# An encoder layer on one core: early sums of squares, a regrouped V for the prompt, V loads in four parts

## The chip, the cores and the metric

The kernel runs on one NeuronCore of one Trainium2 chip, as one launch. The metric is the device time of the launch in microseconds; before the change it is 2137.19 us, the median of three runs (2135.92 to 2137.59).

The engines are named as in the profile: PE is TensorE (PEld its weight loads), DVE is VectorE, ACT is ScalarE, POOL is GpSimd, and SP is SyncE, the engine that issues nearly all DMAs of this kernel, one after the other, on a queue of its own (SPq).

## The reference

One layer of an encoder is applied to a prompt of 512 tokens and to a sample of 2048 tokens, both 1024 wide, in float32 and with shared weights:

```python
def encoder_layer(x, pre_g, post_g, w_in, ...):
    h = rms_norm(x, pre_g)            # x * rsqrt(mean(x*x) + 1e-6) * pre_g
    z = h @ w_in                      # 1024 x (4*512 + 2*256 + 3*256 + 3*1024)
    (q, k, v, gate_a, u_b, gate_b, c_val, c_glu, gate_c,
     merge_a, merge_b, merge_c) = jnp.split(z, split_pts, axis=-1)
    y_a = neighbourhood_attention(heads(q), heads(k), heads(v), rpb) * jax.nn.silu(gate_a)
    y_b = fourier_mix(u_b) * jax.nn.silu(gate_b)
    y_c = conformer_conv(c_val, c_glu, dw_w, dw_b, cn_g, cn_b) * jax.nn.silu(gate_c)
    merged = (jax.nn.sigmoid(merge_a) * (y_a @ w_a) + jax.nn.sigmoid(merge_b) * (y_b @ w_b)
              + jax.nn.sigmoid(merge_c) * (y_c @ w_c))
    return x + rms_norm(merged @ w_o, post_g)
```

The attention sees the tokens as a grid of 64 columns (8 rows for the prompt, 32 for the sample). Each of 8 heads of 64 channels looks at a window of 8 rows by 16 columns, clamped at the border, with a bias by relative position. `fourier_mix` is the real part of a 2-D DFT.

## The kernel before, in words

**Chunks.** The tokens are worked on in five chunks of 512: chunk 0 is the prompt, chunks 1 to 4 are the sample. The order is the chunk pair (1, 2), the pair (3, 4), and then chunk 0 with the merging and the output. A normalized chunk stands in SBUF as eight tiles `hT` of 128 channels by 512 tokens, each split in two parts of a reduced float format, high and low. The weights come in units of 128 x 1024 through `wraw` (three buffers) and are split in the same way into `w` by a cast on ACT and a subtraction on DVE (`split`, L134 and L135). A product is then three matmuls, high by high, high by low and low by high (`narrow`, L178 to L180): 24 matmuls for a block of 512 columns, and one unit serves both chunks of a pair. `unit` keeps three units ready.

**How other work gets among the matmuls.** The projections and the merging run through TensorE in program order. Everything else is a generator that is handed to `task` with a number of steps and a first and last position; after every few matmuls `pump` moves the position on and takes as many steps as are due. The program's order is not the final one: a scheduler of the tile framework orders each engine's instructions by its own model of time, so that where an instruction ends up on DVE, ACT, POOL and SP is seen only in the built program.

**The normalization.** For chunks 1 and 2 the raw x is multiplied and the norm is applied to the products. For chunks 3, 4 and 0 the generator `produce` runs `rstd_rows` and then `make_h`. `rstd_rows` (L199) loads four tiles `xt` of 128 tokens by 1024 through the buffers of `wraw`, squares each on ACT with a sum (L207), gets the reciprocal root by Newton steps on DVE (L126 to L128) and writes it to the DRAM row `rs` (L211). `make_h` (L213) reads that row back, broadcast over the partitions, into `rrow` (L217, one buffer), loads eight tiles `xr` of x transposed (L220, three buffers), multiplies each by `preg` and `rrow` on DVE (L221) and splits it into an `hT`. `produce` of chunks 3 and 4 is a task late in the first pair, that of chunk 0 one late in the second. The tiles of chunk 4 and of chunk 0 take over the eight buffers `ring` of chunk 2 and of chunk 4, those of chunk 3 ten buffers `ring2`.

**The attention.** `attention` (L503) goes over 8 heads and, in each, four blocks `cb` of 16 columns of queries. A block has `nq` x 128 keys: nq is 2 for the prompt, 3 for chunks 1 and 4, 4 for chunks 2 and 3. Per block there are two matmuls for the scores s, a bias (the table `tab` plus a mask, added on POOL at L560 or L563 and made a block ahead), on DVE the sum of both with its maximum (L596), on ACT the exponential (L600), the scaling (L602), then the transposes `pt` (L623), their split into `psp` (L626), and the product `pv` with V (L634), whose halves go into `ob` (L637 and after) and with the last block to DRAM as `ya` (L644, two writes). V comes by `load_v` (L534) at the start of the third block of a head, into `vsp` (two buffers). With nq 4, `grouped`, it takes 8 loads of 16 rows by 8 columns (L540); otherwise 16 loads of 32 keys for nq row groups (L545), four for each block. The prompt's attention runs beside `fft` for chunk 0, which loads `fu` (L664), makes `fab` of it on DVE (L656) and multiplies with the DFT matrix `w` (loaded at L730, 128 x 2048, one buffer; product `hp` at L750).

Of the kernel before, what the change touches and what calls it, by code (L numbers as in the profile page):

```python
# [20 lines left out]
ALU = mybir.AluOpType  # L21
# [13 lines left out]
MASKPAT = (0, 1, 2, 2, 3)  # L35
KSTART = (0, 8, 24, 32)
RCOL = (16, 8, 8, 0)
COLPAT = (0, 1, 1, 2)


def attention_masks():


    out = np.full((4, P, 3, 512), -1e30, np.float32)
    for mp, (rows, r0, kr0, nq) in enumerate(((8, 0, 0, 2), (32, 0, 0, 3), (32, 8, 4, 4), (32, 24, 20, 3))):
        for cp, cb in enumerate((0, 1, 3)):
            for q in range(P):
                r, c = r0 + q // 16, 16 * cb + q % 16
                rs = min(max(r - 4, 0), rows - 8)
                cs = min(max(c - 8, 0), 48)  # L50
                kr = kr0 + np.arange(nq * 4)[:, None]
                kc = KSTART[cb] + np.arange(32)[None, :]
                ok = (kr >= rs) & (kr < rs + 8) & (kc >= cs) & (kc < cs + 16)
                m = np.where(ok, 0.0, -1e30)
                if nq == 4:
                    m = m.reshape(16, 4, 8).transpose(1, 0, 2)
                out[mp, q, cp, : nq * 128] = m.reshape(-1)
    return out.astype(ml_dtypes.bfloat16)

# [44 lines left out]
class Build:  # L104
# [91 lines left out]
                self.pump()  # L196


    def rstd_rows(self, c, pool, xpool, tag, bufs):  # L199

        nc = self.nc
        ss = pool.tile([P, 4], F32, tag="ss", name="ss")
        for i in range(4):
            xt = xpool.tile([P, D], F32, tag=tag, name="xt", bufs=bufs)
            nc.sync.dma_start(xt, self.a["x"][c * C + i * P: c * C + i * P + P, :])
            junk = pool.tile([P, D], BF16, tag="xr", name="junk", bufs=3)
            nc.scalar.activation(junk, xt, AF.Square, accum_out=ss[:, i:i + 1])  # L207
        v = pool.tile([P, 4], F32, tag="v", name="v")
        nc.vector.tensor_scalar(v, ss, 1.0 / D, EPS, op0=ALU.mult, op1=ALU.add)
        r = self.newton(pool, "nr", v, nc.vector)  # L210
        nc.sync.dma_start(self.rs[c].rearrange("o (t p) -> p (o t)", p=P), r)  # L211

    def make_h(self, c, pool, tiles, ring):  # L213

# [289 lines left out]
    def attention(self, c):  # L504
# [2 lines left out]
        nq, trow, krow = PATS[c]  # L507
        n, rows = nq * P, 4 * nq
        kds, vds = self.kds[c > 0], self.vds[c > 0].rearrange("(r w) d -> r w d", w=64)
        grouped = nq == 4  # L510
        mask = pool.tile([P, 3, 512], BF16, tag="mask", name="mask", bufs=1)
        nc.sync.dma_start(mask, self.a["mask"][MASKPAT[c]])
        tq, vq, ahead = [], [], []
# [17 lines left out]
            qk[hh] = ksp, qsp.rearrange("p i (b q) -> p i b q", b=4)  # L531
            tabs[hh] = tb

        def load_v(hh):  # L534

            cols = slice(hh * P, hh * P + P)
            vsp = pool.tile([P, 12, P], F32R, tag="vsp", name="vsp", bufs=2)
            if grouped:
                for g in range(8):
                    nc.sync.dma_start(vsp[:, g].bitcast(F32), vds[krow: krow + rows, 8 * g: 8 * g + 8, cols])  # L540
            else:
                for cb in range(4):
                    for r in range(4):
                        src = vds.rearrange("(q r) w d -> r w q d", r=4)
                        nc.sync.dma_start(  # L545
                            vsp[32 * r: 32 * r + 32, nq * cb: nq * cb + nq].bitcast(F32),
                            src[r, KSTART[cb]: KSTART[cb] + 32, krow // 4: krow // 4 + nq, cols])
            vs[hh] = vsp

        def biases():  # L550
            for hh in range(8):
                for cb in range(4):
                    bias = pool.tile([P, 512], F32, tag="bias", name="bias", bufs=2)
                    g0 = RCOL[cb] // 8
                    t = tabs[hh][:, g0: g0 + 4, trow: trow + rows]
                    m, b = mask[:, COLPAT[cb], :n], bias[:, :n]
                    if grouped:
                        m, b = (x.rearrange("p (g r w) -> p g r w", g=4, w=8) for x in (m, b))
                        m, b, t = (x.rearrange("p g r w -> p g (r w)") for x in (m, b, t))
                        nc.gpsimd.tensor_tensor(b, t, m, op=ALU.add)  # L560
                    else:
                        m, b = (x.rearrange("p (r g w) -> p g r w", g=4, w=8) for x in (m, b))
                        nc.gpsimd.tensor_tensor(b, t, m, op=ALU.add)  # L563
                    yield bias
# [10 lines left out]
        for hh in range(8):  # L575
            ksp, qsp = qk.pop(hh)
            for cb in range(4):
                if cb == 1:
                    load(hh + 1)
                if cb == 2:  # L580
                    load_v(hh)
                if cb % 2 == 0:
                    pv = self.ps.tile([P, 2, 2, P], F32, tag="o", name="pv", bufs=1)
                if cb == 0:
# [3 lines left out]
                s = self.ps.tile([P, 512], F32, tag="s", name="s", bufs=2)  # L588
                kk = ksp.rearrange("p (r c) -> p r c", c=64)[:, :rows, KSTART[cb]: KSTART[cb] + 32]
                if grouped:  # L590
                    kk = kk.rearrange("p r (g w) -> p g r w", w=8)
# [10 lines left out]
                nc.scalar.mul(p[:, :n], p[:, :n], m[:, 3:4])  # L602
                tq.append(partial(self.transpose_p, nq, p, c, hh, cb, vs, pv, obs))
                yield
                if len(tq) > 3:
                    vq.append(tq.pop(0)())
                yield
# [21 lines left out]
    def attend(self, c, hh, cb, nq, vs, psp, pv, obs):  # L629

        nc, vsp, o = self.nc, vs[hh], obs[hh]
        for i in range(nq):
            v = KSTART[cb] // 8 + i if nq == 4 else nq * cb + i
            nc.tensor.matmul(pv[:, cb % 2], lhsT=vsp[:, v], rhs=psp[:, i], start=i == 0, stop=i == nq - 1)  # L634
        if cb % 2 == 0:
            return
        ov = o.rearrange("p (r b c) -> p b r c", r=8, b=4)[:, cb - 1: cb + 1]  # L637
        parts = pv.rearrange("p b i (r c) -> p i b r c", c=16)
        nc.scalar.copy(ov, parts[:, 0])
        nc.vector.tensor_tensor(ov, parts[:, 1], ov, op=ALU.add)  # L640
# [242 lines left out]
    def run(self):  # L883
        tc, nc, a = self.tc, self.nc, self.a
        with ExitStack() as ctx:
# [47 lines left out]

            hT = {c: [] for c in range(NCH)}

            def produce(*cs, x=(self.wraw, "wraw", 3)):
                for c, ring in cs:
                    self.rstd_rows(c, hp, *x)
                    yield
                    yield from self.make_h(c, hp, hT[c], ring)  # L940

            def seq(*gens):
# [33 lines left out]
            second = self.conv(2, cb[2], True)  # L976
            self.task(seq(self.conv(1, cb[1]), islice(second, 20)), 48, base + 20, base + 340)
            self.task(self.dft_parts(), 7, base + 30, base + 200)
            self.proj_qk(hs)
            for g in range(2):  # L980
                self.proj_v(hs, g)
            self.task(self.attention(1), 112, self.pos + 30, self.pos + 270)
            self.proj_u(hs)
            self.gates(hs)
            self.task(produce((3, ring2), (4, ring)), 18, self.pos + 100, self.pos + 292)
            self.merge_gates(hs)
            while len(hT[4]) < KT:
                self.pump()
# [16 lines left out]
            self.task(seq(*(self.attention(c) for c in (2, 3, 4))), 336, self.pos, self.pos + 280)  # L1005
            self.proj_u(hs)
            self.gates(hs)
            self.task(produce((0, ring)), 9, self.pos + 150, self.pos + 232)
            self.merge_gates(hs, turn=True)
            while len(hT[0]) < KT:  # L1010
                self.pump()
# [132 lines left out]
```

## Time and profile before

| | |
|---|---|
| median of three runs | 2137.19 us |
| the profiled execution, its own time | 2136.65 us |
| its span in the trace | 2134.8 us |
| PE busy | 2069.1 us, 97% |
| PEld busy | 1775.8 us, 83% |
| DVE busy | 1300.3 us, 61% |
| ACT busy | 795.8 us, 37% |
| POOL busy | 292.8 us, 14% |
| mean granted clock of TensorE | 0.987 |

The span runs from the first to the last instruction of the trace; the execution's own time is 1.85 us longer. Busy time is a sum over instructions and says nothing of what they waited for. The views read below are the timeline of an engine (each row a run of like instructions, with the idle time before it in brackets and what ended that), the windows (busy time, granted clock and DMA rate of a stretch), and the groups of instructions by line or by tile. The granted clock is given as a share of full speed, 1.00 being 2.4 GHz and 0.50 being 1.2 GHz; a value between is a mean over the stretch. PE is busy for longer in a stretch with a lower clock, for the same work.

### The profile page before, as it was taken

Reading aid. Unit: us, or ns where it says so; the run is one execution under the profiler, and the core shown is the slowest. Engines: PE = TensorE matmul, PEld = TensorE weight load, DVE = VectorE, ACT = ScalarE, POOL = GpSimd, SP = SyncE. Lnnn points to the kernel's source line nnn. Section 1 sums busy time; section 2 is a strip of 40 time slices with the busy share of each in tenths; the row PEclk is TensorE's granted clock in tenths of the full one; section 3 lists DMA queues with packets and bytes.
Section 4 is the critical chain, followed back from the end, with each engine's and each line's share of the span. In section 5 each row is a group of like instructions: output and inputs, shape, how many; then the busy total and the mean of one; then the engine's idle time right before and its main releaser. Section 6 shows DMA issues by size and latency. Waiting matters only on the chain. (4 is left out here: it accounts for less than half of the span.)

```text
span 2134.8 us, 31256 instructions
## 1 busy us (share of the span) xinstructions
PE 2069.1 (97%) x11184; PEld 1775.8 (83%) x11184; DVE 1300.3 (61%) x2850; ACT 795.8 (37%) x1625; POOL 292.8 (14%) x286
## 2 busy tenths in 40 slices
PE   8999999999979999999999969999889999999998
PEld 6889888887867899888888858897778889999997
DVE  6554676556444547686665635887745666666655
ACT  6222243344332215564554635335544311111111
POOL 0000011101000002232221211002100121222211
PEclk9999999999989999999999989999999999999999
DMA  8644444555443536575666676777778765555532
GB/s 299 199 154 162 163 146 147 152 173 159 136 143 115 152 131 177 171 195 173 176 182 185 193 195 193 236 236 219 260 247 300 222 211 173 173 185 171 188 129 77
DMA packets 242091, 389.33 MB, mean 182 GB/s; under 512 B 26784, under 2 KB 140064, under 8 KB 240032
## 3 DMA queue, kind: packets, MB, share of 16 engines
q1 hardware_dynamic: 241936, 387.33, 58.2%
q8 instruction: 89, 1.46, 0.3%
q14 instruction: 66, 0.54, 0.1%
HBM read 284.99 MB, written 109.58 MB: 185 GB/s over the span
## 5 line engine op out<-in xcount | busy, mean ns | idle before, releaser
L178 PE MATMUL mm<-hT,w 128*128 128x512 f32 x1760 | 703.7, 400 | 20.2 <-ACT hT L134 10.9
L180 PE MATMUL mm<-hT,w 128*128 128x512 f32 x1760 | 696.1, 396 | 0.1
L179 PE MATMUL mm<-hT,w 128*128 128x512 f32 x1760 | 695.9, 396 | 0.0
L178 PEld LDWEIGHTS mm<-hT,w 128*128 128x128 f32 x1760 | 333.7, 190 | 88.6 <-ACT hT L134 11.3
L180 PEld LDWEIGHTS mm<-hT,w 128*128 128x128 f32 x1760 | 333.0, 189 | 73.8 <-DVE w L135 1.2
L179 PEld LDWEIGHTS mm<-hT,w 128*128 128x128 f32 x1760 | 333.6, 190 | 66.1 <-DVE hT L242 0.9
L135 DVE TENSOR_TENSOR w<-wraw,w 128x512 fp32r<-128x512 f32 x308 | 222.0, 725 | 176.1 <-ACT w L134 172.3
L134 ACT CAST w<-wraw 128x512 fp32r<-128x512 f32 x308 | 188.5, 618 | 247.3 <-PE mm L180 186.5
L453 DVE SCALAR_TENSOR_TENSOR acc<-cb,cw,acc 128x512 f32<-128x512 f32 (+1 forms) x300 | 237.9, 795 | 2.9
L563 POOL TENSOR_TENSOR bias<-tab,mask 128x384 f32<-128x384 f32 (+1 forms) x96 | 94.3, 984 | 829.7 <-DVE m L596 744.7
L178 PE MATMUL mm<-ysp,wb 128*128 128x256 f32 x640 | 181.1, 283 | 2.7 <-DVE nw_y L116 2.7
L179 PE MATMUL mm<-ysp,wb 128*128 128x256 f32 x640 | 181.0, 283 | 0.0
L180 PE MATMUL mm<-ysp,wb 128*128 128x256 f32 x640 | 180.9, 283 | 0.0
L600 ACT ACTIVATE p<-p,m 128x384 f32<-128x384 f32 (+2 forms) x160 | 102.3, 639 | 184.5 <-DVE m L599 158.6
L596 DVE CUSTOM_DVE_ANT_0 p<-s,bias 128x384 f32<-128x384 f32 (+2 forms) x160 | 92.7, 580 | 86.2 <-PE pt L623 69.2
L560 POOL TENSOR_TENSOR bias<-tab,mask 128x512 f32<-128x512 f32 x64 | 86.1, 1346 | 368.7 <-DVE m L596 356.0
L194 PE MATMUL mm<-w,hT 128*128 128x256 f32 x480 | 134.8, 281 | 0.0
L193 PE MATMUL mm<-w,hT 128*128 128x256 f32 x480 | 134.8, 281 | 0.0
L192 PE MATMUL mm<-w,hT 128*128 128x256 f32 x480 | 134.3, 282 | 0.0
L178 PEld LDWEIGHTS mm<-ysp,wb 128*128 128x128 f32 x640 | 122.4, 191 | 4.3 <-DVE th L831 2.9
L857 PE MATMUL po<-wo,msp 128*128 128x512 f32 x320 | 124.5, 389 | 0.0
L856 PE MATMUL po<-wo,msp 128*128 128x512 f32 x320 | 124.2, 390 | 0.0
(152 smaller groups left out, 2961.7 us busy)
## 6 DMA issues: line engine op xcount, KB each, us to landing
wraw<-wn SPq DMA_DIRECT2D x135, 512.0 KB, 4.5
th<-z SPq DMA_DIRECT2D x120, 256.0 KB, 2.6
th<-th SPq DMA_DIRECT2D x80, 384.0 KB, 3.8
qsp<-qd SPq DMA_DIRECT2D x80, 256.0 KB, 6.2
tab<-tab SPq DMA_DIRECT2D x40, 384.0 KB, 3.9
w<-dftd SPq DMA_DIRECT2D x14, 1024.0 KB, 7.7
vsp<-vds SPq DMA_DIRECT2D x256, 48.0 KB, 2.0
xt<-x SPq DMA_DIRECT2D x20, 512.0 KB, 5.2
```

The lines of the kernel that those rows point to most:

```text
L134: nc.scalar.copy(dst[:, 0], src)
L135: return nc.vector.tensor_tensor(dst[:, 1], src, dst[:, 0].bitcast(F32), op=ALU.subtract)
L178: nc.tensor.matmul(ps, lhsT=u[:, 0, s], rhs=r[:, 0], start=n == 0, stop=False)
L179: nc.tensor.matmul(ps, lhsT=u[:, 0, s], rhs=r[:, 1], start=False, stop=False)
L180: nc.tensor.matmul(ps, lhsT=u[:, 1, s], rhs=r[:, 0], start=False, stop=n == len(kts) - 1)
L192: nc.tensor.matmul(ps, lhsT=r[:, 0, q], rhs=w[:, 0, s], start=kt == 0, stop=False)
L193: nc.tensor.matmul(ps, lhsT=r[:, 0, q], rhs=w[:, 1, s], start=False, stop=False)
L194: nc.tensor.matmul(ps, lhsT=r[:, 1, q], rhs=w[:, 0, s], start=False, stop=kt == KT - 1)
L453: nc.vector.scalar_tensor_tensor(acc[:, :n], cb[:, b, e:e + n], wv[:, e:e + 1], acc[:, :n], op0=ALU.mult, op1=ALU.add)
L600: nc.scalar.activation(p[:, :n], p[:, :n], AF.Exp, bias=m[:, 1:2], accum_out=m[:, 2:3])
L856: nc.tensor.matmul(po, lhsT=r[:, 0, q], rhs=w[:, 0], start=kt == 0, stop=False)
L857: nc.tensor.matmul(po, lhsT=r[:, 0, q], rhs=w[:, 1], start=False, stop=False)
```

## The change

1. `rstd_rows` no longer belongs to `produce`. It is a task of its own, for chunks 3, 4 and 0 in this order, started 20 positions after the first products of chunks 1 and 2 and due by position 200 after them (15 steps). It loads x in halves of 128 x 512 into the three `xr` buffers instead of whole rows into those of `wraw`, squares in place, and adds the two half sums with one more instruction on DVE. `produce` keeps `make_h` alone.
2. The prompt's V is `grouped` too: seven loads of 8 rows by 16 columns (128 keys) that its four blocks share, two blocks each, instead of 16 loads per head. Its keys and its mask are ordered to match, and its bias is added in two POOL instructions of 128 keys.
3. `load_v` works in four parts, two of them in the third block of a head and two in the fourth, for all chunks.

```diff
+VBLOCKS = {4: tuple(range(0, 64, 8)), 2: (0, 16, 8, 24, 40, 32, 48)}
...
-                if nq == 4:
-                    m = m.reshape(16, 4, 8).transpose(1, 0, 2)
+                if nq != 3:
+                    m = m.reshape(4 * nq, nq, 32 // nq).transpose(1, 0, 2)
...
-    def rstd_rows(self, c, pool, xpool, tag, bufs):
+    def rstd_rows(self, c, pool):
 
         nc = self.nc
-        ss = pool.tile([P, 4], F32, tag="ss", name="ss")
+        ss = pool.tile([P, 2, 4], F32, tag="ss8", name="ss8")
         for i in range(4):
-            xt = xpool.tile([P, D], F32, tag=tag, name="xt", bufs=bufs)
-            nc.sync.dma_start(xt, self.a["x"][c * C + i * P: c * C + i * P + P, :])
-            junk = pool.tile([P, D], BF16, tag="xr", name="junk", bufs=3)
-            nc.scalar.activation(junk, xt, AF.Square, accum_out=ss[:, i:i + 1])
+            for k in range(2):
+                xt = pool.tile([P, C], F32, tag="xr", name="xt", bufs=3)
+                row = c * C + i * P
+                nc.sync.dma_start(xt, self.a["x"][row: row + P, k * C: k * C + C])
+                nc.scalar.activation(xt, xt, AF.Square, accum_out=ss[:, k, i:i + 1])
+            yield
         v = pool.tile([P, 4], F32, tag="v", name="v")
-        nc.vector.tensor_scalar(v, ss, 1.0 / D, EPS, op0=ALU.mult, op1=ALU.add)
+        nc.vector.tensor_scalar(v, ss[:, 0], 1.0 / D, EPS, op0=ALU.mult, op1=ALU.add)
+        nc.vector.scalar_tensor_tensor(v, ss[:, 1], 1.0 / D, v, op0=ALU.mult, op1=ALU.add)
...
-        grouped = nq == 4
+        grouped, width = nq != 3, 32 // nq
...
-        def load_v(hh):
+        def load_v(hh, part):
 
             cols = slice(hh * P, hh * P + P)
-            vsp = pool.tile([P, 12, P], F32R, tag="vsp", name="vsp", bufs=2)
+            if part == 0:
+                vs[hh] = pool.tile([P, 12, P], F32R, tag="vsp", name="vsp", bufs=2)
+            vsp, first, last = vs[hh], 2 * part, 2 * part + 2
             if grouped:
-                for g in range(8):
-                    nc.sync.dma_start(vsp[:, g].bitcast(F32), vds[krow: krow + rows, 8 * g: 8 * g + 8, cols])
+                for i, k in enumerate(VBLOCKS[nq][first:last]):
+                    nc.sync.dma_start(vsp[:, first + i].bitcast(F32), vds[krow: krow + rows, k: k + width, cols])
...
+                    elif nq == 2:
+                        for i in range(2):
+                            mi, bi = (x[:, i * P: i * P + P].rearrange("p (r g w) -> p g r w", g=2, w=8)
+                                      for x in (m, b))
+                            nc.gpsimd.tensor_tensor(bi, t[:, 2 * i: 2 * i + 2], mi, op=ALU.add)
...
-                if cb == 2:
-                    load_v(hh)
+                if cb >= 2:
+                    load_v(hh, 2 * cb - 4)
...
                 yield
+                if cb >= 2:
+                    load_v(hh, 2 * cb - 3)
...
-            v = KSTART[cb] // 8 + i if nq == 4 else nq * cb + i
+            v = nq * cb + i if nq == 3 else VBLOCKS[nq].index(KSTART[cb] + 32 // nq * i)
...
-            def produce(*cs, x=(self.wraw, "wraw", 3)):
+            def produce(*cs):
                 for c, ring in cs:
-                    self.rstd_rows(c, hp, *x)
-                    yield
                     yield from self.make_h(c, hp, hT[c], ring)
...
+            self.task(seq(*(self.rstd_rows(c, hp) for c in (3, 4, 0))), 15, base + 20, base + 200)
...
-            self.task(produce((3, ring2), (4, ring)), 18, self.pos + 100, self.pos + 292)
+            self.task(produce((3, ring2), (4, ring)), 16, self.pos + 110, self.pos + 292)
...
-            self.task(produce((0, ring)), 9, self.pos + 150, self.pos + 232)
+            self.task(produce((0, ring)), 8, self.pos + 155, self.pos + 232)
```

What moves is read from the two built programs. Lines of the changed kernel are 2 to 13 higher. First, SP's queue early in the first pair, in the changed program (`xt` are the half rows of x, `rs_100` and `rs_101` the rows of chunks 3 and 4):

```order
L144 DMA wraw<-wn 128x1024 x3
L209 DMA xt<-x 128x512 x3
L144 DMA wraw<-wn 128x1024 x2
L209 DMA xt<-x 128x512 x3
L144 DMA wraw<-wn 128x1024
L209 DMA xt<-x 128x512 x2
L1100 DMA cdf<-cdft 128x256
L209 DMA xt<-x 128x512 x3
L144 DMA wraw<-wn 128x1024
L209 DMA xt<-x 128x512 x7
L216 DMA rs_100<-nw_y 128x4x1
```

The loads of x stand among those of the weights from here to the third row rs, that of chunk 0, 25 rows on; before the change there are weights alone in this place.

Second, SP's queue before the second pair, around the tiles of chunk 4, in the changed program (`rrow<-rs_101` is chunk 4's, `rrow<-rs_97` chunk 0's; `th` are writes of merge gates):

```order
L226 DMA xr<-xT 128x512 x3
L223 DMA rrow<-rs_101 128x512
L444 DMA th_93<-z 128x512
L226 DMA xr<-xT 128x512 x3
L144 DMA wraw<-wn 128x1024
L444 DMA th_94<-z 128x512
L226 DMA xr<-xT 128x512
L144 DMA wraw<-wn 128x1024
L226 DMA xr<-xT 128x512 x2
L444 DMA th_94<-z 128x512
L226 DMA xr<-xT 128x512 x4
L223 DMA rrow<-rs_97 128x512
```

Chunk 0's row is read here, some 600 us of the old trace ahead of its old place, and its first three `xr` follow those of chunk 4.

Third, SP's queue in chunk 0's attention and DFT, before the change:

```order
L545 DMA vsp<-vdp 32x2x128 x4
L644 DMA ya_82<-ob 64x512 x2
L545 DMA vsp<-vdp 32x2x128 x6
L500 DMA yd_77<-th 128x512
L545 DMA vsp<-vdp 32x2x128 x6
L530 DMA tab<-tab 128x768
L664 DMA fu<-ud_72 128x4x128
```

and the same place in the changed program:

```order
L548 DMA vsp<-vdp 128x1x128 x3
L657 DMA ya_82<-ob 64x512 x2
L548 DMA vsp<-vdp 128x1x128 x4
L677 DMA fu<-ud_72 128x4x128
L506 DMA yd_77<-th 128x512
```

Between the writes of `ya` and the load of `fu` there are four V loads where there were twelve, a write and a table.

## Rows read from the trace of the kernel before

**Rows 1.** Timeline of PE, waits over 2 us, 400 to 1620; start, length, instruction, [idle <-releaser]

```profile
500.33 0.98 PE L634 MATMUL pv<-psp,vsp 128*128 128x256 f32 x3 [2.34 <-issue]
...
630.55 0.79 PE L178 MATMUL mm<-hT,w 128*128 128x512 f32 x1 [10.89 <-ACT hT L134]
...
1278.48 0.88 PE L623 MATMUL pt<-ident,p 128*128 128x128 f32 x3 [16.09 <-DVE m L599]
...
1544.18 0.69 PE L623 MATMUL pt<-ident,p 128*128 128x128 f32 x2 [7.90 <-DVE psp L626]
...
1584.91 0.44 PE L623 MATMUL pt<-ident,p 128*128 128x128 f32 x2 [2.08 <-ACT p L602]
...
1590.31 1.01 PE L750 MATMUL hp<-w,fgs 128*128 128x256 f32 x3 [3.65 <-DMA w<-dftd]
```

**Rows 2.** Windows: length, busy PE, PEld, DVE, ACT, POOL, PEclk, DMA share, GB/s

```profile
500.00:505.00 5.00, 4.67 (x15) 3.90 (x16) 4.52 (x9) 1.76 (x4) 0.32 (x1) 0.66 0.48 137
630.00:640.00 10.00, 9.40 (x28) 7.04 (x29) 7.55 (x12) 3.60 (x6) 0.00 (x0) 0.66 0.29 84
1280.00:1285.00 5.00, 5.00 (x23) 4.23 (x22) 3.19 (x11) 3.01 (x7) 0.97 (x2) 0.81 0.63 165
1545.00:1550.00 5.00, 5.00 (x18) 3.97 (x17) 3.05 (x14) 2.98 (x9) 1.36 (x2) 0.68 1.01 383
1590.00:1595.00 5.00, 4.69 (x14) 4.02 (x15) 0.72 (x2) 0.40 (x1) 0.00 (x0) 0.50 0.83 302
```

**Rows 3.** Timeline of DVE, its waits ahead of those of PE

```profile
483.59 0.75 DVE L221 SCALAR_TENSOR_TENSOR xr<-xr,preg,rrow 128x512 f32<-128x512 f32 x1 [10.11 <-DMA rrow<-rs]
...
629.09 1.41 DVE L221 SCALAR_TENSOR_TENSOR xr<-xr,preg,rrow 128x512 f32<-128x512 f32 x2 [12.38 <-DMA rrow<-rs]
...
1274.20 1.41 DVE L221 SCALAR_TENSOR_TENSOR xr<-xr,preg,rrow 128x512 f32<-128x512 f32 x2 [19.58 <-DMA rrow<-rs]
...
1543.03 0.76 DVE L656 TENSOR_TENSOR fab<-fu 128x256 f32<-128x256 f32 x2 [9.93 <-DMA fu<-ud]
```

**Rows 4.** Timeline of SP's queue ahead of C

```profile
1255.60 12.21 SPq L545 DMA_DIRECT2D vsp<-vds  x11
...
1268.33 0.43 SPq L217 DMA_DIRECT2D rrow<-rs  x1
```

**Rows 5.** Timeline of SP's queue ahead of D1 and D2

```profile
1527.83 2.07 SPq L644 DMA_DIRECT2D ya<-ob  x2
...
1533.80 4.34 SPq L545 DMA_DIRECT2D vsp<-vdp  x6
...
1538.66 0.43 SPq L664 DMA_DIRECT2D fu<-ud  x1
...
1574.25 4.59 SPq L545 DMA_DIRECT2D vsp<-vdp  x7
```

**Rows 6.** Timeline of ACT at D2

```profile
1583.83 0.62 ACT L134 CAST w<-wraw 128x512 fp32r<-128x512 f32 x1 [6.05 <-DMA wraw<-wn]
```

**Rows 7.** Instructions of the tile xr, all of the span

```profile
DMA to landing us min/median/max: 2.6/4.6/10.4
```

**Rows 8.** Windows of the early stretch and of chunk 0's attention, columns as in rows 2

```profile
60.00:150.00 90.00, 90.00 (x408) 73.93 (x407) 47.00 (x71) 19.91 (x32) 0.21 (x1) 1.00 0.62 191
1440.00:1535.00 95.00, 93.36 (x485) 77.08 (x484) 77.56 (x215) 55.91 (x144) 19.47 (x21) 1.00 0.76 238
```

**Rows 9.** Instructions of the tile xt, all of the span: ns min/median/max, first and last start

```profile
L207 ACT ACTIVATE junk<-xt x12: 1052/1057/1082, 446.7 to 1241.5; 128x1024 bf16<-128x1024 f32 x12
...
DMA to landing us min/median/max: 3.5/5.2/11.5
```

**Rows 10.** Instructions of the tile wraw, 20 to 120: ended its engine's idle time, us, times

```profile
  PE mm L180: 26.7, 16
```

**Rows 11.** Groups by line and form, POOL, 1300 to 1620: busy us, mean ns

```profile
L563 POOL TENSOR_TENSOR bias<-tab,mask 128x256 f32<-128x256 f32 x32 | 27.5, 863 | 235.9 <-DVE m L596 216.3 <-DVE m L601 11.3 <-DMA vsp<-vdp 7.4
```

**Rows 12.** Instructions of the tile wraw, 1440 to 1535

```profile
L135 DVE TENSOR_TENSOR w<-wraw,w x26: 666/686/957, 1440.5 to 1530.7; 128x512 fp32r<-128x512 f32 x26
```

More of the change, by code (lines that the diff above doesn't have):

```diff
@@ L196, in wide @@
                 self.pump()
-    def rstd_rows(self, c, pool, xpool, tag, bufs):
+    def rstd_rows(self, c, pool):
         nc = self.nc
-        ss = pool.tile([P, 4], F32, tag="ss", name="ss")
+        ss = pool.tile([P, 2, 4], F32, tag="ss8", name="ss8")
         for i in range(4):
-            xt = xpool.tile([P, D], F32, tag=tag, name="xt", bufs=bufs)
-            nc.sync.dma_start(xt, self.a["x"][c * C + i * P: c * C + i * P + P, :])
-            junk = pool.tile([P, D], BF16, tag="xr", name="junk", bufs=3)
-            nc.scalar.activation(junk, xt, AF.Square, accum_out=ss[:, i:i + 1])
+            for k in range(2):
[4 more added lines that the diff above has]
+            yield
         v = pool.tile([P, 4], F32, tag="v", name="v")
-        nc.vector.tensor_scalar(v, ss, 1.0 / D, EPS, op0=ALU.mult, op1=ALU.add)
+        nc.vector.tensor_scalar(v, ss[:, 0], 1.0 / D, EPS, op0=ALU.mult, op1=ALU.add)
+        nc.vector.scalar_tensor_tensor(v, ss[:, 1], 1.0 / D, v, op0=ALU.mult, op1=ALU.add)
         r = self.newton(pool, "nr", v, nc.vector)
         nc.sync.dma_start(self.rs[c].rearrange("o (t p) -> p (o t)", p=P), r)
+        yield
     def make_h(self, c, pool, tiles, ring):
@@ L532, in load @@
             tabs[hh] = tb
-        def load_v(hh):
+        def load_v(hh, part):
             cols = slice(hh * P, hh * P + P)
-            vsp = pool.tile([P, 12, P], F32R, tag="vsp", name="vsp", bufs=2)
+            if part == 0:
+                vs[hh] = pool.tile([P, 12, P], F32R, tag="vsp", name="vsp", bufs=2)
+            vsp, first, last = vs[hh], 2 * part, 2 * part + 2
             if grouped:
-                for g in range(8):
-                    nc.sync.dma_start(vsp[:, g].bitcast(F32), vds[krow: krow + rows, 8 * g: 8 * g + 8, cols])
-            else:
[L542 to L548, printed above, removed]
+                for i, k in enumerate(VBLOCKS[nq][first:last]):
+                    nc.sync.dma_start(vsp[:, first + i].bitcast(F32), vds[krow: krow + rows, k: k + width, cols])
+            else:
+                for r in range(4):
+                    src = vds.rearrange("(q r) w d -> r w q d", r=4)
+                    nc.sync.dma_start(
+                        vsp[32 * r: 32 * r + 32, nq * part: nq * part + nq].bitcast(F32),
+                        src[r, KSTART[part]: KSTART[part] + 32, krow // 4: krow // 4 + nq, cols])
         def biases():
@@ L556, in biases @@
                     m, b = mask[:, COLPAT[cb], :n], bias[:, :n]
-                    if grouped:
+                    if nq == 4:
                         m, b = (x.rearrange("p (g r w) -> p g r w", g=4, w=8) for x in (m, b))
@@ L590, in attention @@
                 if grouped:
-                    kk = kk.rearrange("p r (g w) -> p g r w", w=8)
+                    kk = kk.rearrange("p r (g w) -> p g r w", w=width)
                 nc.tensor.matmul(s[:, :n], lhsT=qsp[:, 0, cb], rhs=kk, start=True, stop=False)
```

## The prediction

> **What bounds the kernel now.** I read the page's busy times first: TensorE is busy 2069.1 of 2134.8 us, so all that any change in scheduling can win is the remaining 65.7 us plus what the lowered clock costs. The chain of waits that ended last is nearly all TensorE. So I went along TensorE's timeline and took every wait of over 2 us between 400 and 1620 us [rows 1]; the waits at the start lie before anything that the change touches. There are five such places, and I call them A (500 us), B (630), C (1278), D1 (1544) and D2 (1585 and 1590). Behind each wait the granted clock is low for 5 or 10 us [rows 2]: with a clock of 0.50, half of the busy time would not have been needed at full speed. A stretch thus loses busy time × (1 − PEclk): 4.67 × 0.34 = 1.6 at A, 9.40 × 0.34 = 3.2 at B, 5.00 × 0.19 = 0.95 at C, 5.00 × 0.32 = 1.6 at D1, 4.69 × 0.50 = 2.3 at D2. Wait and clock together:
>
> - A 2.34 + 1.6 = 3.9 us
> - B 10.89 + 3.2 = 14.1 us
> - C 16.09 + 0.95 = 17.0 us
> - D1 7.90 + 1.6 = 9.5 us
> - D2 2.08 + 3.65 + 2.3 = 8.0 us
>
> Together 52.5 us. Now what stands behind them. In A, B and C it is VectorE, and VectorE itself waits: 10.11, 12.38 and 19.58 us for rrow, the row of reciprocal norms that `make_h` reads back from DRAM [rows 3]. All three are the product of `rstd_rows` running just ahead of `make_h`: loads, squares, Newton steps, a write, a read, all in one line, while VectorE's order already has the multiplication by rrow next. At C one sees where most of the time goes: between the write of rs and the read into rrow, eleven V loads hold SP's queue for 12.21 us, and the read goes out only at 1268.33 [rows 4]. At D1 VectorE waits 9.93 us for fu [rows 3], the load of which is issued at 1538.66, behind two ya writes and twelve V loads, the last six of which take 4.34 us [rows 5]. At D2 a weight load goes out behind seven V loads, which take 4.59 us [rows 5], and ScalarE's cast waits 6.05 us for it [rows 6]; the wait of 3.65 us is for the DFT matrix w, a load of 1 MB into a single buffer.
>
> **The change, part by part.** *The sums of squares come early.* The rs rows of chunks 3, 4 and 0 are then written in the first 110 us or so. What is left of the line at A, B and C is one load of rrow, which can go out as soon as its buffer is free. Of the waits in [rows 3] the part that is rs is gone at A and at C: 3.9 and 17.0 us. At B the rest is a pace: three xr buffers feed eight tiles of chunk 4, and the order also puts chunk 0's three multiplications, which need rrow a third time, near the first cb of the next pair. Loading (median 4.6 us [rows 7]), multiplying (0.75 [rows 3]) and splitting (0.7, as VectorE's other subtractions of this form) three tiles takes about 4.6 + 0.75 + 0.7 = 6 us, so eight tiles take three such turns, some 18 us. Their buffers in the ring are read for the last time by the last block of chunk 2, and two blocks of chunk 3 stand between that and the first use of chunk 4, which was due at 630.55 − 10.89 = 619.7. A block is 24 matmuls, 24 × 90/408 = 5.3 us [rows 8], so the ring comes free from about 604 on, the eighth tile is ready near 622 and wanted at 619.7 + 7 × 0.66 = 624.3: about 2 us to spare. I take 13 of B's 14 us.
>
> What the moved work costs there: 24 half-row loads of 256 KB in place of 12 of 512 KB, 24 squares in place of 12. A whole square takes 1057 ns [rows 9], a half lies between 0.53 and 1.06, each with its read of the accumulator (0.19): 24 × 0.72 to 24 × 1.25 = 17 to 30 us of ScalarE between 60 and 150 us, where it is busy 19.9 of 90 us [rows 8]: 50 of 90 at most. VectorE gets one tiny instruction more per chunk and is busy 47 of 90 us. The loads go through three buffers; a turn is a landing (4.6 us) and a square (0.8) and its issue (0.4), so 24 loads take about 5.8/3 × 24 = 46 us. On SP they stand between six weight loads; in this stretch the casts wait 26.7 us for TensorE and for no load of wraw [rows 10], so weights are there ahead of time: `unit` keeps three units ready, and each serves two blocks of 5.3 us, one per chunk. Cost: nothing on the path. If that cover fails it is the slower rival below.
>
> *V of the prompt in seven blocks.* Per head, 16 loads become 7, 56 instead of 128 over eight heads; by [rows 5] six take 4.34 us, or 0.72 each, so SP gets 128 × 0.72 − 56 × 0.72 = 52 us back in the stretch from 1415 to 1615. At D1 the new order has the two ya writes, then four V loads, then fu: 4 × 0.72 = 2.9 us after ya, where it was 1538.66 − (1527.83 + 2.07) = 8.8. So fu comes 5.9 us earlier; VectorE's wait falls from 9.93 to about 4.0, and TensorE's from 7.90 to 2.0, with which the clock's 1.6 should go too. I take 7.5 of D1's 9.5. At D2 the seven V loads ahead of the weights are gone, with that the 2.08; the DFT matrix has the same single buffer, and I give half of 3.65 + 2.3 back, from neither to all: 2.08 + 3.0 = 5 of 8.0, bounds 2 and 8.
>
> The price: GpSimd adds the prompt's bias in two instructions. The 32 whole ones take 27.5 us [rows 11]; 64 halves cost between half (0.43 each, nothing more) and whole (0.86, 27.5 us more); I take the middle, 14. GpSimd is busy 19.5 of 95 us there [rows 8] and its instructions are issued a block ahead, so nothing lies on the path. For VectorE's share of it: its subtraction for the weights takes 666 ns at the least, 686 in the median and 957 at most in the stretch where GpSimd works [rows 12], so that few of them are held up at all. I put 0.5 us on contention. The Trainium skill speaks against this part: GPSIMD Engine Reference, section 1 (Specifications), says that GpSimd shares its SBUF interfaces with VectorE and contends with VectorE instructions that have two SBUF inputs, which these subtractions are. By it, taken in full, VectorE would lose the added 14 us in the stretch and most of D's gain would go; the median, 20 ns above the least, does not bear that out.
>
> *V loads in four parts* changes when loads are issued, not how many (chunks 1 to 4: 16 or 8 as before). Each part is issued seven generator steps or more before the product that reads it (a product comes five blocks of three steps after its scores), and the tightest task spreads 336 steps over 280 pump positions of six matmuls, 1.3 us: 1.1 us a step, over 7 in all. xr, a load of 256 KB and so no smaller, lands in 4.6 us in the median and 10.4 at most [rows 7]. It takes runs of eleven V loads on SP apart [rows 4]; nothing is counted for it beyond C. If its cover is gone, the product pv waits some 2 us per head at most in places, which the upper end holds.
>
> **Sum:** A 3.9 + B 13 + C 17.0 + D1 7.5 + D2 5 = 46.4, less 0.5: 46 us. The profiled execution took 2136.65 (its span 2134.8), 0.5 below the median of the runs, 2137.19: 2136.65 − 46 ≈ **2091 us**.
>
> **Rivals.**
> 1. *D keeps its stalls.* VectorE, not SP, could be what D waits for: it is busy 77.6 of 95 us there [rows 8], and fab only moves up as far as its own order lets it; w's single buffer stays as it is. Then only A, B and C go: 3.9 + 13 + 17.0 = 33.9, 2103 us. The named row "fu" as VectorE's releaser speaks against it [rows 3]. Chance 0.22. The Trainium skill's rule on the shared interfaces (GPSIMD Engine Reference, section 1) would lead to this time too.
> 2. *B's wait comes back in part.* Three xr buffers set the pace, and a multiplication of chunk 0 that waits for rrow blocks what follows on VectorE, cb among it: some 6 us of wait and 2 of clock stay, 2091 + 8 = 2099. The ring's place in the order speaks for it; the 2 us to spare against. Chance 0.15.
> 3. *Slower: the early loads starve TensorE.* Each xt on SP waits for its buffer, and six weight loads queue behind. The six units carry 6 × 2 × 5.3 = 64 us of products and the three ready ones 32 more, together 96. With a landing of L the 24 loads take 24 × (L + 1.2)/3; at 11.5 us, the longest landing of xt [rows 9], that is 102 us against 96 and costs 6, which still leaves a gain; at 18 us it is 153 and costs 57, which outweighs 46: 2136.65 − 46 + 57 ≈ 2148. It decides from a landing of some 17 us on, which no row shows: chance 0.04.
> 4. *The moved steps end where they did*, since the scheduler delays them: 2137. The new order, with all three rs writes long ahead, speaks against it: chance 0.02.
>
> **The numbers.** The forecast has 0.57. Low end: all of the 52.5, 2084, and a quarter of the idle time that [rows 1] do not hold (65.7 − 42.95 = 22.8), since V loads are shorter on SP all along: 2078. High end: rival 1 with the 6 us of rival 3 or of late V parts, 2110. Within 0.2% (4.3 us, about what measurements of this kernel can tell) of before lies rival 4. Faster 0.94 (forecast, rivals 1 and 2), same 0.02, slower 0.04.
>
> **What would show it.** Right: no wait of VectorE for rrow above 4 us and no TensorE wait near 500 and 1278 us; fu issued within 4 us of ya; the rs writes before 120 us and no TensorE wait there. Wrong: a TensorE wait for hT at the start of the second pair of over 5 us (rival 2), VectorE waiting 8 us or more for fu or TensorE for the DFT's w (rival 1), casts waiting for wraw before 150 us (rival 3).

## The result, and the profile after

The changed kernel takes 2080.37 us, median of four runs (2078.99 to 2082.26), against 2136.56 for the kernel before (2132.54 to 2137.59, four runs). The ratio is 0.9741, with a 95% interval of 0.9724 to 0.9758: 56 us faster, where 46 had been forecast, with 2091 us and a range of 2078 to 2110. The profiled execution took 2078.99 us, its span is 2077.2.

The page's first lines, of the changed kernel (engine, busy us, share of the span, instructions):

```profile
span 2077.2 us, 31264 instructions
PE 2050.4 (99%) x11184; PEld 1773.8 (85%) x11184; DVE 1296.3 (62%) x2853; ACT 801.3 (39%) x1649; POOL 301.6 (15%) x318
```

TensorE now idles for 26.8 us of its span, where it was 65.7. All that it waits for by name is in four rows (the waits of PE: who, for whom, us in total, times, the longest):

```profile
PE mm L180 <- ACT w L136: 7.1, 2, 5.9
PE mm L180 <- DVE z L319: 6.6, 2, 4.4
PE mm L180 <- DVE nw_y L118: 3.8, 1, 3.8
PE mm L180 <- DVE nw_t L128: 1.3, 1, 1.3
```

None of the six waits of [rows 1] is left. The first row lies at the start, as before; the second and the fourth are new, and lie between 80 and 111 us; the third is in the merging, where the kernel before waits 2.7 us for the same Newton steps.

What stood behind the old waits is read from VectorE's timeline. These are the longest waits for rrow, for x and for fu that are left at B, C and D1, to be held against the 12.38, 19.58 and 9.93 us of [rows 3]:

```profile
626.56 1.42 DVE L227 SCALAR_TENSOR_TENSOR xr<-xr,preg,rrow 128x512 f32<-128x512 f32 x2 [2.05 <-DMA rrow<-rs]
...
1279.52 0.75 DVE L227 SCALAR_TENSOR_TENSOR xr<-xr,preg,rrow 128x512 f32<-128x512 f32 x1 [2.27 <-DMA xr<-xT]
...
1483.89 0.76 DVE L669 TENSOR_TENSOR fab<-fu 128x256 f32<-128x256 f32 x2 [1.67 <-DMA fu<-ud]
```

And SP's queue ahead of D1, the answer to [rows 5]:

```profile
1474.66 1.29 SPq L657 DMA_DIRECT2D ya<-ob  x2
1476.87 3.56 SPq L548 DMA_DIRECT2D vsp<-vdp  x4
1480.53 0.40 SPq L677 DMA_DIRECT2D fu<-ud  x1
```

The load of fu goes out 1480.53 − (1474.66 + 1.29) = 4.6 us after the writes of ya, where it was 8.8.

**Where the time came from, and where some of it went.** TensorE's projections stand in the same order in both programs, so the n-th matmul into `mm` can be matched with the n-th of before, and the difference of their starts, each from the start of its trace, is the time won or lost up to there. By stretches of the trace before:

| stretch (us of before) | change against before | the prediction's term |
|---|---|---|
| 46 to 146, the early sums | +8.6 | 0 |
| 470 to 588, A | −5.0 | −3.9 |
| 588 to 668, B | −16.2 | −13 |
| 1208 to 1314, C | −18.7 | −17.0 |
| 1512 to 1570, D1 | −10.9 | −7.5 |
| 1570 to 1653, D2 | −12.1 | −5 |
| 1653 to 1743, merging | +3.0 | none |
| all other stretches | −6.0 | +0.5 (contention) |
| sum | −57.3 | −46 |

So the change won 69 us and lost 11.6 of them again, 8.6 in a place where the forecast had put no cost. The other 3.0, in the merging, lie within what that stretch shows over the twelve runs below (−0.3 to +3.9, and +2.3 in `p3_parts`); that the change costs them is not shown. The borders of the last stretches are not sharp either: matmuls of the attention and the DFT stand between those that are matched, and in the changed program 20 more of them fall in the 198 us ahead of D1, 4 fewer in D1 and 16 fewer in D2. Those three stretches together gain 25.5 us.

Where the 8.6 us are lost the chain is this, in four rows of VectorE, ScalarE and TensorE:

```profile
78.32 0.17 DVE L128 TENSOR_TENSOR nw_t<-nw_y 128x4 f32<-128x4 f32 x1 [7.69 <-DMA rs<-nw_y]
...
93.55 0.63 ACT L210 ACTIVATE xt<-xt 128x512 f32<-128x512 f32 x1 [10.25 <-DMA xt<-x]
...
94.81 0.69 DVE L137 TENSOR_TENSOR w<-wraw,w 128x512 fp32r<-128x512 f32 x1 [10.78 <-ACT w L136]
...
96.25 0.77 PE L180 MATMUL mm<-hT,w 128*128 128x512 f32 x1 [4.42 <-DVE z L319]
```

VectorE wants to begin the Newton steps of chunk 4, but the two buffers of that tag are taken until the write of chunk 3's rs row has landed; then ScalarE has a square next, whose x has not landed; and behind the square, at 94.18 us, stands a cast of weights that uses nothing of it. VectorE's subtraction for the same weights follows at 94.81, and behind that z, for which TensorE has waited.

### The profile page after: what moved, and what is told of

Read it like the earlier page. It is cut to its first block, busy times and chain, and to the rows that moved or that the text cites. A ratio compares the mean times of both kernels' runs of the same rounds, so it can differ in the third digit from the quotient of the medians.

```text
span 2077.2 us, 31264 instructions
## 1 busy us (share of the span) xinstructions
PE 2050.4 (99%) x11184; PEld 1773.8 (85%) x11184; DVE 1296.3 (62%) x2853; ACT 801.3 (39%) x1649; POOL 301.6 (15%) x318
## 5 line engine op out<-in xcount | busy, mean ns | idle before, releaser
L574 POOL TENSOR_TENSOR bias<-tab,mask 128x384 f32<-128x384 f32 x64 | 67.4, 1056 | 572.1 <-DVE m L607 529.4
```

## The experiments

All twelve were run beside the kernel before. The place called "early loss" is the first stretch of the table above, read in each run's trace in the same way.

### One part at a time

`p1_sums` is the kernel before with the new `rstd_rows`, its task and the shorter `produce`, and V as it was.

> Only the early sums of squares; V is loaded as before. By the trace of the change, matched matmul by matmul with that of before, the change loses 9 us between 80 and 125 us and wins about 5 at A, 16 at B and 18 at C. Theory (the three parts act in their own places): this kernel shows just these, 2137 - 39 + 9 = 2107 us, with D1 and D2 as before. Rival (the burst of eleven V loads at C is held up for its own reason, and the parts are needed there): C keeps 8 us or more of its wait and the time is 2115 or more.

Measured: 2106.07 us, ratio 0.9855 (0.9829 to 0.9881). A −5.0, B −16.2, C −18.7, as in the change, and the early loss is 16.6 us. At D1 and D2 TensorE waits nearly as before (the two longest waits of PE from 1400 to 1660 us):

```profile
PE pt L627 <- DVE psp L630: 6.2, 2, 5.9
PE hp L754 <- DMA w<-dftd: 3.5, 1, 3.5
```

The gain at C did not need the loads in parts: a run of twelve V loads still stands there on SP, and nothing waits behind it that TensorE needs.

```profile
1255.44 5.53 SPq L549 DMA_DIRECT2D vsp<-vds  x12
```

`p2_blocks` has the prompt's seven V loads, its mask and bias, loaded at once, and the old sums.

> Only the prompt's V in seven blocks, loaded at once. Theory: D1 and D2 win what they do in the change, 22 us in place of the 12.5 of the prediction: 2115 us, A, B and C as before. Rival (D's gain needs the loads in parts, or work that chunk 0's product no longer does there): 12 us or less, 2125 or more.

Measured: 2115.31 us, ratio 0.9901 (0.9878 to 0.9923). D1 −11.0 and D2 −12.1 us, all of the change's gain there. A, B and C keep their waits (the three longest waits of PE from 400 to 1650 us):

```profile
PE pt L631 <- DVE m L607: 17.3, 1, 17.3
PE mm L180 <- ACT hT L136: 10.6, 1, 10.6
PE pv L642 <- issue: 2.3, 1, 2.3
```

`p3_parts` changes only when the V loads are issued:

```diff
-                if cb == 2:
-                    load_v(hh)
+                if cb >= 2:
+                    load_v(hh, 2 * cb - 4)
...
                 yield
+                if cb >= 2:
+                    load_v(hh, 2 * cb - 3)
```

> Only load_v in four parts. Theory: nothing that can be measured beyond A's small pv wait, 2132 to 2138 us. Rival (runs of eleven V loads on SP are part of C's and D's waits): C's and D1's waits shrink by 5 us or more together, 2130 or less.

Measured: 2134.09 us, ratio 0.9979 (0.9966 to 0.9993): 1.5 to 7 us faster by that interval, and its profiled execution shows 4.7 won at D1 and given back before and after. C's and B's waits are whole, 16.4 and 11.5 us.

`p12_noparts` is the change with all four parts of V issued together at the start of the third block.

> The change without its third part: early sums and V in blocks, V loaded at once. Theory: the terms add up, p1 and p2 together, 2080 to 2086 us. Rival (the parts carry gain in the presence of the others): 2090 or more, with a wait of PE for pv or psp that the change has not.

Measured: 2079.40 us, ratio 0.9734 (0.9710 to 0.9757), not to be told from the change. What the first two parts win adds up, 0.9855 × 0.9901 = 0.976, and with them in place nothing is left for the third. The early loss is 11.6 us here. On SP, ScalarE and VectorE the early work stands in the same order in p1_sums, p12_noparts and the change, so 16.6, 11.6 and 8.6 us are three outcomes of one order. How long a transfer takes varies: from the issue of the load of x that goes out at 80 to 81 us to its square it is 7.4, 7.0 and 13.2 us in the three. It also means that a few us between the early losses of single traces, below, are no finding.

### What the early loss is

Four theories in turn, each with an edit of a line or two. First the Newton buffers, and what the DMAs around them do:

```diff
-        r = self.newton(pool, "nr", v, nc.vector)
+        r = self.newton(pool, "nr", v, nc.vector, bufs=4)
```

> The change, with four buffers instead of two for the Newton tiles of the sums. Theory (the early loss of 9 us begins with VectorE, which waits 7.7 us for the write of chunk 3's rs row to land before it may reuse that buffer, and with it the weight subtraction behind it): that wait and the TensorE waits after it go, 2072 to 2076 us. Rival (the loss is the volume of the 24 loads, or the write in SP's queue): VectorE's wait goes but the casts wait for the loads all the same, 2078 to 2082.

Measured: 2079.88 us, ratio 0.9734 (0.9718 to 0.9750). VectorE's wait of 7.69 us is gone, the early loss is still 8.0: the rival, as far as the time goes. A square waits for a load of x that is issued right behind chunk 4's rs write, and starts 11.7 us after that issue (SP's queue, then ScalarE):

```profile
82.79 0.56 SPq L216 DMA_DIRECT2D rs<-nw_y  x1
83.39 1.94 SPq L209 DMA_DIRECT2D xt<-x  x2
...
95.12 0.63 ACT L210 ACTIVATE xt<-xt 128x512 f32<-128x512 f32 x1 [8.10 <-DMA xt<-x]
```

`f2_rsq` issues the rs writes with `nc.gpsimd.dma_start`, `f3_both` does both.

> The change, with the three rs writes (512 pieces of 4 bytes each) issued on GpSimd's queue instead of SP's. Theory: the write lands sooner, since no x loads share its queue, but VectorE still waits for it; a part of the loss goes, 2074 to 2079 us. Rival (SP's queue is held up by the write itself, and that is the whole loss): 2071 to 2074, and no load of x lands later than 6 us.

Measured: 2082.77 us, ratio 0.9742 (0.9725 to 0.9759); early loss 11.5 us. Neither came about: on GpSimd's queue chunk 4's write goes out at 81.10 us, a load of x on SP's at 82.2, and the square that waits 8.80 us for it starts 14.2 us after that.

> Four Newton buffers and the rs writes on GpSimd's queue. Theory: the early loss falls from 9 us to under 3: 2070 to 2074 us. Rival (volume of the loads): 2078 or more, with ScalarE's squares waiting for xt as before.

Measured: 2083.38 us, ratio 0.9748 (0.9728 to 0.9767); early loss 11.3 us. The theory fell here: neither the buffer nor the queue of the write decides.

`f4_dft` moves the copies of the DFT matrices:

```diff
-            self.task(self.dft_parts(), 7, base + 30, base + 200)
+            self.task(self.dft_parts(), 7, base + 200, base + 370)
```

> The change, with the copies of the DFT matrices (dft_parts, 1 MB each from DRAM to DRAM) moved from base+30..200 to base+200..370, away from the early loads. Theory (the Newton buffer starts the loss, the DFT copy only lengthens it, by the 6.7 us that a load of x waits for it on SP): the second TensorE wait of 4.4 us goes, the first of 1.3 stays, 2074 to 2077 us. Rival (the copy plays no part): 2079 to 2082.

Measured: 2079.86 us, ratio 0.9732 (0.9717 to 0.9747); early loss 9.3 us, the rival. SP's wait of 6.7 us for the copy went, but a square still waits 8.76 us, for a load that goes out 0.7 us after chunk 4's write. In `f5_xtact` ScalarE issues the x loads of `rstd_rows` itself (`nc.scalar.dma_start`), so that they share no queue with Q and K.

> The change, with the 24 early loads of x issued by ScalarE itself instead of SP. The four runs before this one left the early loss at 8 to 13 us, and in all of them a square on ScalarE waits 8 to 9 us near 95 us for a load of x that SP issues late, after an issue for Q or K (ksp, qd) on which SP itself waits. Theory (two queues in order hold each other: weight casts stand behind the square on ScalarE, the square's load behind Q's and K's transfers on SP): the wait at 95 us goes, the early loss falls from 9 to 4 us or less, 2072 to 2076 us. Rival (the loads' volume): the squares wait as long as before, 2079 or more.

Measured: 2078.68 us, ratio 0.9739 (0.9726 to 0.9753); early loss 10.8 us. The square still waits, with nothing of SP's ahead of its load (ScalarE, 86.99 us):

```profile
86.99 0.63 ACT L210 ACTIVATE xt<-xt 128x512 f32<-128x512 f32 x1 [8.00 <-DMA xt<-x]
```

So "two queues hold each other" fell too. Its premise was read wrongly: when the n-th load is matched with the n-th square, the loads that are waited for had not been issued late. This one went out at 73.5 us, 0.1 us after chunk 3's rs write, and its square starts 13.5 us later.

`f8_c0after` has the four Newton buffers, early sums for chunks 3 and 4 alone, and chunk 0's behind chunk 4's tiles:

```diff
-            self.task(seq(*(self.rstd_rows(c, hp) for c in (3, 4, 0))), 15, base + 20, base + 200)
+            self.task(seq(*(self.rstd_rows(c, hp) for c in (3, 4))), 10, base + 20, base + 200)
...
-            self.task(produce((3, ring2), (4, ring)), 16, self.pos + 110, self.pos + 292)
+            self.task(seq(produce((3, ring2), (4, ring)), self.rstd_rows(0, hp)), 21, self.pos + 110, self.pos + 292)
```

> The change with four Newton buffers, and chunk 0's sums (8 of the 24 loads and squares) ordered behind chunk 4's tiles instead of early. Theory (only the loads that meet Q's and K's transfers on SP cost, the last eight): early loss 3 us or less, and up to 3 us lost at the start of the second pair, where the eight loads now stand: 2071 to 2077 us. Rival (the loss comes with the first loads too): 2079 or more.

Measured: 2077.97 us, ratio 0.9736 (0.9723 to 0.9750); early loss 8.7 us. A third of the loads is gone from the place, and the loss is not. Another instruction stands in the way: with the xr buffers free sooner, the scheduler brings chunk 3's multiplication forward to where the squares were, and VectorE waits there for rrow, whose read had to wait for the rs write (VectorE's timeline in this run):

```profile
87.32 1.42 DVE L227 SCALAR_TENSOR_TENSOR xr<-xr,preg,rrow 128x512 f32<-128x512 f32 x2 [10.96 <-DMA rrow<-rs]
```

> Both: x loaded by ScalarE, chunk 0's sums behind chunk 4's tiles, four Newton buffers. Theory: early loss under 2 us, 2070 to 2075 us. Rival (issuing on ScalarE costs as much as it saves): slower than the run with chunk 0's sums moved alone.

`f9_c0after_act`, the same with x loaded by ScalarE: 2081.66 us, ratio 0.9751 (0.9738 to 0.9764), early loss 9.3 us, with the same wait for rrow, 12.1 us. That is on the rival's side, but the two intervals overlap: not to be told apart.

### The pace of the early sums

In those runs, whichever wait was taken away, the next one in the same 20 us took its place; and the longest of them stand behind an rs write of 65 to 90 us, in all runs but the change itself. Over the eleven kernels with early sums there are 15 loads of x, each waited for by a square (waits over some 0.3 us are counted), that go out within 5 us after an rs write: the square starts 9.8 to 14.2 us after the issue, on whichever queue either of them was issued. For the 102 other loads that a square waits for it is 4.4 us in the median, and over 8.5 in 5 of them. One of the five is the change's own wait of 10.25 us: its load goes out at 80.32 us, 11 us after chunk 3's rs write and right behind a copy of a DFT matrix. Writing rs in larger pieces was not tried.

The last experiment leaves all 24 loads and squares in, and holds the loads back to the pace of their task, each behind the weight load that is the last one at that point of the program; also the read of chunk 3's rrow. The four Newton buffers are in it too.

```diff
-                nc.sync.dma_start(xt, self.a["x"][row: row + P, k * C: k * C + C])
+                with self.tc.issue_after(self.load.ins):
+                    nc.sync.dma_start(xt, self.a["x"][row: row + P, k * C: k * C + C])
...
-        nc.sync.dma_start(rrow, self.rs[c].to_broadcast([P, C]))
+        with self.tc.issue_after(self.load.ins) if c == 3 else ExitStack():
+            nc.sync.dma_start(rrow, self.rs[c].to_broadcast([P, C]))
```

> The change with four Newton buffers, and with each load of x for the sums, and the read of rrow for chunk 3, issued only behind the weight load that is the last one at its place in the program; so 24 loads and squares stand at the pace at which their task is stepped, from about 70 to about 330 us, instead of as early as three buffers allow (40 to 100 us). The seven runs before it left TensorE 7 to 13 us late by 125 us, each by another wait: what they share is a square or a multiplication at 80 to 97 us that stands in an in-order queue ahead of the weight casts and of z, and waits 8 to 11 us for a transfer. Theory (it is the crowding of sums, Q and K transfers in 70 to 100 us, not any single wait): the early loss falls under 2 us, A, B and C keep their gain, 2068 to 2074 us. Rival (24 loads and squares cost what they cost wherever they stand): the loss turns up along 70 to 330 us, 2078 or more.

Measured: 2072.47 us, median of five runs (2069.6 to 2073.2), ratio 0.9705 (0.9691 to 0.9719), whose interval lies below that of the change; its slowest run lies below the fastest of all the others, 2076.19. By its trace the early stretch wins 0.5 us instead of losing 8.6, and A, B, C and D win what they do in the change. The rs writes go out at 123, 216 and 292 us. The windows from 60 to 150 us, of the change and then of this run (length; busy us of PE, PEld, DVE, ACT, POOL with their instructions; clock, DMA share, GB/s):

```profile
60.00:150.00 90.00, 82.10 (x354) 66.99 (x353) 49.85 (x108) 28.32 (x62) 0.21 (x1) 0.98 0.80 221
```

```profile
60.00:150.00 90.00, 90.00 (x407) 74.28 (x406) 50.12 (x86) 25.97 (x49) 0.21 (x1) 1.00 0.76 217
```

TensorE runs through with 407 matmuls, as the kernel before had 408 [rows 8]. The squares now start over a stretch of 226 us, and they take as long as in the change, where it is 613 to 634 ns (tile xt of this run: ns min/median/max, first and last start):

```profile
L210 SPq DMA_DIRECT2D xt<-x x24: 328/428/1517, 58.5 to 283.3; - x24
L211 ACT ACTIVATE xt<-xt x24: 616/632/636, 62.9 to 288.5; 128x512 f32<-128x512 f32 x24
```

So the loss was neither the number of the loads nor the squares. Nor is it the sum of their waits: here ScalarE waits 30.9 us ahead of squares, in 16 waits of 5.2 us at most, where it waits 25.6 us in 11 in the change, once for 10.25. And it is not how much moves at that time: from 70 to 100 us the DMA engines move 270 GB/s here, 168 in the change and 230 in the kernel before. The rs writes have not become quicker either: behind the last one, from 298 to 303 us, the DMA engines are busy for 0.99 of the time and move 39 GB/s, and TensorE does not wait. What is left is that squares which waited for late transfers stood in the order ahead of work that TensorE needed. The late transfers are mostly those near the rs writes, as far as the traces show. The pacing moves the loads and the rs writes away from 70 to 100 us together; a run that holds back only the rs writes was not made, so which of the two counts is open. What the pacing of rrow brings was not tried apart either; the four buffers alone bring nothing that shows (`f1_nr4`).

## Why the prediction was right, and where it was not

**The total** came out because terms that were too small outweighed a cost that was left out: −69 us where the sum had 46.4, less 11.6 of losses. That it lies in the range is in part luck: `f10_paced`, the change with the early loads paced and without the early loss, lies at 2072, below the low end of 2078.

**A and C** were sized rightly. With rs written by 117 us, rrow is there, and −5.0 and −18.7 us stand against 3.9 and 17.0. One reading was wrong: the prediction laid most of C's line to eleven V loads on SP, between the write of rs and the read. In the trace of before that write, issued at 1254.40 us, lands 11.1 us later, so the read could not go out before 1265.5, and of the 12.21 us of V loads at most 2.8 were in its way. At A and B, where the writes land after 9.1 and 7.5 us, the read goes out at once. p1_sums and p3_parts agree: it is the early rs that frees C, while V loads in parts leave its wait at 16.4 us; and the twelve V loads at 1255 us hold nothing up once no read of rrow stands behind them.

**B** was under-sized, 13 against 16.2. The "2 us to spare" held: VectorE still waits for x and rrow around 600 to 627 us, 2.05 us at most, and TensorE does not. Of the 2.1 us that were left out, 0.8 is a small wait at 651 us; the rest was not found.

**D1 and D2** were under-sized most: 7.5 and 5 against 10.9 and 12.1 us. At D1 the step "VectorE's wait falls from 9.93 to about 4.0" was too careful; fu came 4.6 us after ya, not 2.9, yet the wait is 1.67. VectorE now begins to wait 6.3 us after the ya writes, where it was 3.2, and fab starts 3.4 us after fu's issue, where it was 4.4. At D2 the step that failed is "I give half of 3.65 + 2.3 back": the single buffer of the DFT matrix, which had not changed, did not cost anything any more once the work ahead of it was in time. p2_blocks shows that the blocks alone do this; p1_sums, with the old loads, still has 3.5 us of it. The 25.5 us of D1, D2 and the stretch ahead of them are more than the whole 17.5 that the prediction found there: before, TensorE idles 16.2 us in them, of which [rows 1] hold 13.6, and in the change not at all; the rest, clock and a slower pace behind the waits, was not split further.

**"Cost: nothing on the path"**, for the early loads, was wrong by 8.6 us. The count behind it was right: 24 halves took 631 ns each, within its bounds, and the weights had a cover of some 96 us in total. What it missed is the order on each engine: the cast at 94.18 us, which uses nothing of the square, starts only behind it. A cover that is large in sum is no cover for the one cast that stands behind one late square. Rival 3 named the place and the queue, but priced it by the volume over 100 us; f8 and f9, with a third of the loads gone, show that volume has little to do with it, and f10, with all 24 loads, that their place has.

**The price of GpSimd** was nearly met: 64 halves take 36.6 us, 9.1 more than the 27.5 of [rows 11], where 14 were taken:

```profile
L571 POOL TENSOR_TENSOR bias<-tab,mask 128x128 f32<-128x128 f32 x64 | 36.6, 595 | 206.1 <-DVE m L607 192.4 <-DMA mask<-mask 8.8 <-DVE m L612 4.8
```

In 95 us of the prompt's attention (1385 to 1480 us) GpSimd is busy 28.3 us, where it was 19.5 [rows 8]; in 1404 to 1499 us, which by the matched matmuls is the stretch of [rows 8], it is 27.7. VectorE's subtraction takes no longer in the median than in [rows 12]:

```profile
L137 DVE TENSOR_TENSOR w<-wraw,w x28: 667/684/850, 1388.9 to 1476.9; 128x512 fp32r<-128x512 f32 x28
```

So the first rival, that D keeps its stalls, has nothing left to stand on. The median hides that the two engines do get in each other's way. Of the 308 such subtractions of a trace, 58 overlap a GpSimd instruction, and all that take over 705 ns are among these: 25 before, the longest 1809 ns, and 23 in the change, the longest 1796. Of the 250 that overlap none, none takes over 703. Above 690 ns each, those long ones add up to 11.1 us before and 9.6 in the change, so the added instructions of GpSimd cost nothing here. The Trainium skill's rule on the interfaces that GpSimd shares with VectorE (GPSIMD Engine Reference, section 1) says that such subtractions are contended for; the trace agrees, but few are, and no more than before.

**V in four parts** was counted at nothing beyond the others; it is worth 0.1 to 0.3% alone and nothing that shows beside them.

**The signs that were named:** rs by 120 us, rrow's waits under 4, no wait at 500 and 1278 us came true; fu within 4 us of ya was missed by 0.6; "no TensorE wait" near the early sums was the one that failed.

## What to carry to other kernels

A chain of small steps (sum, write, read back) that runs just ahead of its use costs all of its latency; moved to where nobody waits, it can cost none, as in `f10_paced`, and what it frees can be larger than the waits that carry its name. But work that is moved "where the engine is idle" must be checked for what stands behind it in the order of each engine and queue, not for its sum: hold it to a pace, rather than let it run as early as its buffers allow. When three repairs of a stall each bring up the next wait in the same place, stop repairing waits and move the crowd.

## What the runs showed of the hardware

A write of 2 KB in 512 pieces of 4 bytes was slow out of proportion: chunk 3's rs goes out on SP at 69.34 us, and VectorE is released by it at 78.32, 9.0 us later, while xr loads of 256 KB took 4.6 us in the median [rows 7]. Where the landing itself is on record, the three writes of the kernel before land 7.5 to 11.1 us after their issue, those of `p1_sums` 10.4 to 11.2, and those of `f2_rsq`, on GpSimd's queue, 9.8 to 14.6.

```profile
69.34 0.39 SPq L216 DMA_DIRECT2D rs<-nw_y  x1
```

In the transfers of the change between 66 and 100 us, in 40 slices of 0.85 us, one sees it as slices in which hardly anything moves (busy share in tenths, then GB/s); those from 75 to 79 us have 2 GB/s:

```profile
DMA  3897489996701000149900699763020046868999
GB/s 51 299 313 243 75 249 216 229 130 17 22 2 2 2 2 0 34 140 839 761 0 0 263 371 329 124 137 24 14 29 0 10 39 234 282 55 147 335 418 418
```

The Trainium skill (DMA: Bandwidth & Descriptors, Specifications) puts the least size for full rate at 512 bytes and says that below it the engines read, modify and write; the row agrees in kind, though what share of the 9.0 us that is no run here shows. Such slices also lie behind the rs writes of `f10_paced` (from 127 to 132 us 40 GB/s, with the DMA engines busy 0.83 of the time). Moving that write to another queue did not make the kernel faster, and loads of x behind it were late on SP's queue and on ScalarE's.
